# Moving a query convolution and its chunk products ahead of a block inverse, and keeping that inverse by columns

## The chip, the cores and the metric

One core of one Trainium2 chip runs the whole kernel. The metric is the device time of one execution in microseconds; three executions of the kernel before took 2511.12, 2511.8 and 2515.66 us, median 2511.8 us.

## The reference, cut to what matters

Two transformer blocks follow each other over 1024 tokens of width 1024. The first one normalizes x, projects it with `w_in`, and from the projection feeds a windowed attention and a bidirectional gated delta rule (4 heads of 128, two directions). The second block is untouched by the change. What the change touches is the front of the delta rule:

```python
qkv = silu(centred_conv(qkv, conv_w))            # 5 taps, per channel
q, k, v = split(qkv, 3);  q, k = l2norm(q), l2norm(k)
decay = exp(where(causal, gc[:, None] - gc[None, :], -inf))
kk    = einsum("cd,sd->cs", k, k)
a_mat = where(strict, beta[:, None] * kk * decay, 0)
t_mat = solve_triangular(eye + a_mat, eye)       # the inverse
qk    = einsum("cd,sd->cs", q, k) * decay
```

A serial scan over chunks then uses `t_mat`, `qk`, keys and values in each direction.

## The kernel before, in words

All matrix products of the first block keep fp32 accuracy by splitting both operands into a high and a low part and running three products (`mm3`, lines 147 to 149). Weights come in through `raw` (3 buffers), are split by ACT and POOL (lines 98 and 99) into `wh` and `wl` (8 buffers each). The kernel leaves the order of the instructions on each engine to a planner at build time, which starts from the order of the program and its own estimate of times; at run time every engine and every DMA queue works strictly in that order. SP issues the loads (`dma`), ACT issues the stores (`put`).

The order of the program, around the change:

- Lines 261 to 267 normalize eight row tiles of 128 tokens. Each tile is loaded (`hx`), scaled by DVE (line 180), transposed by PE (line 183) and split into `XN` (lines 186, 187). Tiles 0 to 3 make the first half of the tokens, 4 to 7 the second.
- Lines 351 to 356 make the 16 gate columns for each half (line 355), and lines 363 to 399 turn them into the gates `G`; the running sums go to `gc_d` in DRAM.
- `project(c0, epi)` multiplies `XN` with 512 columns in two groups of 256. It holds four weight pairs a group, so the next group is loaded while one is used. Its epilogue for keys, queries and values is `conv_epi`: both halves of 128 channels are collected in a tile `cv` (4 buffers), then for each half four or five DVE taps (lines 292, 294), a sigmoid (lines 156 to 159) and a product on POOL (line 297); the result is stored to `gk_d`, `gq_d` or `gv_d`.
- Line 412 projects the keys. Lines 415 to 424 make the decay of each of 8 chunks in a tile `e` (2 buffers), from a broadcast load of `gc_d`, and store it to `e_d`.
- Lines 431 to 456, for each chunk: load the keys (`kT`), transpose them (line 435), multiply keys with keys (line 448), load `e` back, form `b` (line 454) and store it to `key_d`.
- Lines 459 to 478, for each direction: load the 32x32 diagonal blocks `U` of all 32 chunk-heads and invert them on DVE by 31 pairs of a product (line 473) and a sum (line 475). The product reads the finished part of `X` transposed, so that its inner step is 32 elements. The inverses go to `inv_d`.
- Line 480 projects attention's keys and values, line 502 the values, lines 503 to 511 transpose them by chunk. Line 512 projects the queries and lines 513 to 524 load `kT`, `qT` and `e` again for each chunk, multiply keys with queries (line 517) and store the decayed product to `qry_d`.
- Lines 552 to 668 are the scan: `invert` widens the inverses to 128x128, `advance` runs the states of both directions. It stands before lines 670 and 671, the projections of attention's queries and of z, and before the attention (lines 677 to 737). The planner puts these products between the steps of the scan.

Of the kernel before, what the change touches and what calls it, by code (L numbers as in the profile page):

```python
# [9 lines left out]
F32 = mybir.dt.float32  # L10
# [7 lines left out]
P = 128  # L18
T = 1024
# [37 lines left out]
def tile_hybrid_layers(ctx, tc, a, out):  # L57
# [19 lines left out]
    def scratch(name, shape):  # L77
        return dr.tile(shape, F32, name=name, tag=name)
# [82 lines left out]
    def rstd_of(halves):  # L161
        st = sm.tile([P, 8], F32, name="st", tag="st")
        for j in range(2):
            act.activation(junk, halves[j], AF.Square, accum_out=st[:, j : j + 1])
        return rstd_from(st)
# [37 lines left out]
    line_d, wide_d = scratch("line_d", [8, 512]), scratch("wide_d", [8, P, 512])  # L203
    gc_d, eg_d = scratch("gc_d", [64, P]), scratch("eg_d", [64, P])
    kv_d = scratch("kv_d", [8, 2, P, 512])
    e_d = scratch("e_d", [8, 2, P, 512])

    xbq_d = [[scratch(f"{n}{d}_d", [8, 4, P, P]) for d in range(2)] for n in ("inv", "key", "qry")]

# [19 lines left out]
    def bank():  # L229
        return pg.tile([P, 512], F32, name="g", tag="g")  # L230
# [27 lines left out]
    XU = units(xp, "xn")  # L258
    XN = kts(XU)
    wb = ip.tile([P, T], F32, name="wb", tag="U", bufs=2)  # L260
    for i in range(8):
        hx = cvp.tile([P, T + 4], F32, name="cv", tag="cv")[:, :T].rearrange("p (j c) -> p j c", j=2) if 0 < i < 5 else up_tile("e", 2)
        hv = [hx[:, j, :] for j in range(2)]
        dma(hx, a["x"][0][i * P : (i + 1) * P, :].rearrange("p (j c) -> p j c", j=2))
        if i == 0:
            dma(wb, a["norm_mix_w"][0].partition_broadcast(P))
        to_units(hv, rstd_of(hv), i, wb, XU, [bank(), bank2()])


    cur = {}  # L270
# [65 lines left out]
    raw = wp.tile([P, 512], F32, name="raw", tag="raw", bufs=3)  # L336
    dma(raw[:, 0:P].rearrange("p (k m) -> p k m", k=8), W1[:, 2816:2832].rearrange("(k p) m -> p k m", p=P))

    WAB = wp.tile([P, 512], F32R, name="wh", tag="wh", bufs=8)[:, 0 : 2 * P].rearrange("p (k s m) -> p k s m", k=8, s=2)
    split(WAB[:, :, 0], WAB[:, :, 1], raw[:, 0:P].rearrange("p (k m) -> p k m", k=8), gp)  # L340
    cr = tmp()
    dma(cr[:60, 0:P], a["conv_w"][0].rearrange("t (j p) -> (t j) p", p=P))
# [66 lines left out]
    def by_head(x):  # L409
        return x.rearrange("p (h c) -> p h c", h=4)  # L410

    project(1280, conv_epi(1, gk_d))


    for c in range(8):
        e = up_tile("e", 2)
        g4 = gc_d.rearrange("(d c h) t -> c d (h t)", d=2, c=8)[c]
        dma(e, g4.partition_broadcast(P))
        for d in range(2):
            for h in range(4):  # L420
                dve.scalar_tensor_tensor(e[:, d, hs(h)], e[:, d, hs(h)], G["gc"][:, d, c, h : h + 1], neg[d],
                                         op0=ALU.subtract, op1=ALU.min)
            act.activation(e[:, d], e[:, d], AF.Exp)
        put(e_d[c].rearrange("d i j -> i d j"), e)


    z4 = ip.tile([P, P], F32, name="z4")
# [1 line left out]
    for d in range(2):  # L429
        dma(xbq_d[0][d].rearrange("c h i j -> i (c h) j"), z4.unsqueeze(1).to_broadcast([P, 32, P]))  # L430
    for c in range(8):
        kT = chunk_of(gk_d, c, "kT")
        ps = bank()
        for h in range(4):
            pe.transpose(ps[:, hs(h)], kT[:, hs(h)], ident)
        kt = up_tile("kt")
        act.copy(kt, ps)
        put(kv_d[c, 0], kt)
        for h in range(4):
            act.activation(junk[:, 0:P], kt[:, hs(h)], AF.Square, accum_out=SS[:, c, h : h + 1])  # L440
        dve.tensor_scalar(SS[:, c], SS[:, c], EPS, None, op0=ALU.add)
        dve.reciprocal(R2[:, c], SS[:, c])
        gp.tensor_tensor(NR[:, c], SS[:, c], phalf.to_broadcast([P, 4]), op=ALU.pow)
        for d in range(2):
            dve.tensor_mul(G["br"][:, d, c], G["beta"][:, d, c], R2[:, c])
        kk = bank2()
        for h in range(4):
            pe.matmul(kk[:, hs(h)], kT[:, hs(h)], kT[:, hs(h)], start=True, stop=True)
        e = up_tile("e", 2)
        dma(e, e_d[c].rearrange("d i j -> i d j"))  # L450
        b = up_tile("b", 2)
        for d in range(2):
            for h in range(4):
                dve.scalar_tensor_tensor(b[:, d, hs(h)], kk[:, hs(h)], G["br"][:, d, c, h : h + 1], e[:, d, hs(h)],
                                         op0=ALU.mult, op1=ALU.mult)
            put(xbq_d[1][d][c].rearrange("h i j -> i h j"), by_head(b[:, d]))


    for d in range(2):
        U = ip.tile([P, 32, 32], F32, name="U", tag="U", bufs=2)  # L460
        X = ip.tile([P, 32, 32], F32, name="X", tag="X", bufs=2)
        M = ip.tile([P, 31, 31], F32, name="M", tag="M", bufs=2)
        for b in range(4):
            r = slice(32 * b, 32 * b + 32)
            dma(U[r], xbq_d[1][d].rearrange("c h i j -> (c h) i j")[:, r, r])
        dve.tensor_scalar(U, U, -1.0, None, op0=ALU.mult)
        gp.memset(X, 0.0)
        gp.memset(X.rearrange("p i j -> p (i j)")[:, 0:1024:33], 1.0)
        for s in range(1, 32):
            i = 31 - s if d == 0 else s  # L470
            r = slice(i + 1, 32) if d == 0 else slice(0, i)
            m = M.rearrange("p a b -> p (a b)")[:, : s * s].rearrange("p (a b) -> p a b", a=s)
            dve.tensor_tensor(m, U[:, i, r].unsqueeze(1).to_broadcast([P, s, s]),
                                             X[:, r, r].rearrange("p j c -> p c j"), op=ALU.mult)
            dve.tensor_reduce(X[:, i, r], m, axis=AX.X, op=ALU.add)
        for b in range(4):
            r = slice(32 * b, 32 * b + 32)
            dma(xbq_d[0][d].rearrange("c h i j -> (c h) i j")[:, r, r], X[r])

    dense(W1, 512, 2, XN, kv_epi, by_half=True)  # L480

# [16 lines left out]
        act.copy(t, ps)  # L498
        put(zs_d[m * P : (m + 1) * P, h * 512 : (h + 1) * 512], t)

    PV, PQ, PZ, PA = (1792, conv_epi(2, gv_d)), (768, conv_epi(0, gq_d)), (2304, z_epi), (0, q_epi)
    project(*PV)
    for c in (0, 7, 1, 6, 2, 5, 3, 4):
        vT = chunk_of(gv_d, c, "kT")
# [4 lines left out]
        for h in range(4):  # L509
            act.activation(t[:, hs(h)], ps[:, hs(h)], AF.Copy, scale=NR[:, c, h : h + 1])  # L510
        put(kv_d[c, 1], t)
    project(*PQ)
    for c in (0, 7, 1, 6, 2, 5, 3, 4):
        kT, qT = chunk_of(gk_d, c, "kT"), chunk_of(gq_d, c, "qT")
        ps = bank2()
        for h in range(4):
            pe.matmul(ps[:, hs(h)], kT[:, hs(h)], qT[:, hs(h)], start=True, stop=True)
        e = up_tile("e", 2)
        dma(e, e_d[c].rearrange("d i j -> i d j"))
        for d in range(2):  # L520
            for h in range(4):
                dve.scalar_tensor_tensor(e[:, d, hs(h)], ps[:, hs(h)], G["br"][:, d, c, h : h + 1], e[:, d, hs(h)],
                                         op0=ALU.mult, op1=ALU.mult)
            put(xbq_d[2][d][c].rearrange("h i j -> i h j"), by_head(e[:, d]))
    s1.close()

    s2 = ctx.enter_context(ExitStack())
# [745 lines left out]
```

## Time and profile before

| | us |
|---|---|
| median of three executions | 2511.8 |
| profiled execution, its own time | 2522.66 |
| span from its first to its last instruction | 2520.9 |
| PE busy | 2384.3 (95%) |
| DVE busy | 1285.9 (51%) |
| ACT busy | 1074.3 (43%) |
| POOL busy | 928.8 (37%) |

The profiled execution is 10.9 us longer than the median. PE is TensorE's matrix work, PEld its weight loads, DVE VectorE, ACT ScalarE, POOL GpSimd, SP SyncE. Times in the rows count from the first instruction; an entry in square brackets is the idle time of the engine before the instruction and what ended it.

### The profile page before, as it was taken

The page shows a single profiled execution, that of the slowest core. Times are in us where ns is not written, and L with a number is a line of the kernel's source. Part 1 is how long each engine was busy: PE and PEld are TensorE (multiplying, and loading weights), DVE is VectorE, ACT ScalarE, POOL GpSimd, SP SyncE. Part 2 cuts the span into 40 slices and gives each one's busy share as a digit, 9 for nine tenths or more (in the row PEclk, how much of TensorE's full clock was granted, in tenths as well). Part 3 has the DMA queues.
Part 4 walks back from the last instruction along what each step waited for, and adds up shares of the span by engine and source line. Part 5 has one row for each costly group of instructions (what it writes and reads, how often), then busy time and mean ns, then how long its engine had stood idle before and what let it go on. Part 6 is the DMA issues. An engine that isn't in the chain of part 4 may idle for free. (4 is left out here: it accounts for less than half of the span.)

```text
span 2520.9 us, 31629 instructions
## 1 busy us (share of the span) xinstructions
PE 2384.3 (95%) x11098; PEld 1954.2 (78%) x11098; DVE 1285.9 (51%) x2481; ACT 1074.3 (43%) x2185; POOL 928.8 (37%) x799
## 2 busy tenths in 40 slices
PE   7899888899999999999999999998999999999998
PEld 5677677887788888888888788777777787888887
DVE  5579936885632211221123504999888885312113
ACT  5554215664542233223224423666555575333331
POOL 3344224434332222222223214455444442345354
PEclk9999988999999999999999999999999999999999
DMA  5895795656221111111112324122222225312123
GB/s 164 226 286 170 214 289 159 195 150 203 73 69 57 42 43 51 50 50 51 50 51 92 103 89 121 57 76 66 66 67 64 71 80 171 113 51 84 51 72 121
DMA packets 307282, 268.47 MB, mean 106 GB/s; under 512 B 44871, under 2 KB 240387, under 8 KB 307123
## 3 DMA queue, kind: packets, MB, share of 16 engines
q1 hardware_dynamic: 264403, 213.41, 29.6%
q10 hardware_dynamic: 42720, 53.05, 6.1%
q8 instruction: 87, 1.43, 0.2%
q14 instruction: 72, 0.59, 0.1%
HBM read 203.92 MB, written 64.57 MB: 107 GB/s over the span
## 5 line engine op out<-in xcount | busy, mean ns | idle before, releaser
L99 POOL TENSOR_TENSOR wl<-raw,wh 128x512 fp32r<-128x512 f32 x276 | 370.8, 1355 | 834.8 <-ACT wh L98 808.9
L147 PE MATMUL mm<-uh,wh 128*128 128x512 f32 x1472 | 578.3, 393 | 0.2 <-DVE mx L1066 0.2
L149 PE MATMUL mm<-uh,wl 128*128 128x512 f32 x1472 | 576.9, 392 | 0.0
L148 PE MATMUL mm<-ul,wh 128*128 128x512 f32 x1472 | 576.4, 392 | 0.0
L98 ACT CAST wh<-raw 128x512 fp32r<-128x512 f32 (+1 forms) x277 | 169.9, 618 | 460.9 <-PE mm L149 239.3
L149 PEld LDWEIGHTS mm<-uh,wl 128*128 128x128 f32 x1472 | 277.7, 189 | 59.5
L147 PEld LDWEIGHTS mm<-uh,wh 128*128 128x128 f32 x1472 | 278.1, 189 | 55.0 <-DVE mx L1066 0.6
L148 PEld LDWEIGHTS mm<-ul,wh 128*128 128x128 f32 x1472 | 277.8, 189 | 55.4
L99 DVE TENSOR_TENSOR hid<-t,hid 128x512 fp32r<-128x512 f32 x64 | 55.4, 866 | 310.1 <-ACT hid L98 310.1
L149 PE MATMUL mm<-wh,hid 128*128 128x512 f32 x512 | 199.0, 389 | 0.0
L148 PE MATMUL mm<-wl,hid 128*128 128x512 f32 x512 | 198.8, 389 | 0.0
L147 PE MATMUL mm<-wh,hid 128*128 128x512 f32 x512 | 198.7, 389 | 0.0
L845 DVE TENSOR_TENSOR h<-h,mm 128x512 f32<-128x512 f32 x128 | 87.9, 687 | 212.3 <-PE mm L149 212.2
L1015 POOL TENSOR_TENSOR ul<-u,uh 128x512 fp32r<-128x512 f32 (+3 forms) x96 | 106.1, 1106 | 134.5 <-DVE uh L1014 108.5
L147 PE MATMUL mm<-xnh,wh 128*128 128x512 f32 x352 | 142.6, 405 | 11.1 <-ACT cv L280 5.8
L110 POOL TENSOR_TENSOR wl<-raw,wh 128x512 fp32r<-128x512 f32 x72 | 101.6, 1411 | 120.7 <-DVE wh L109 45.2
L148 PE MATMUL mm<-xnl,wh 128*128 128x512 f32 x352 | 141.8, 403 | 0.0
L149 PE MATMUL mm<-xnh,wl 128*128 128x512 f32 x352 | 141.4, 402 | 0.0
L148 PEld LDWEIGHTS mm<-wl,hid 128*128 128x128 f32 x512 | 96.1, 188 | 20.0
L147 PEld LDWEIGHTS mm<-wh,hid 128*128 128x128 f32 x512 | 96.1, 188 | 20.0
L149 PEld LDWEIGHTS mm<-wh,hid 128*128 128x128 f32 x512 | 96.1, 188 | 19.9
L830 ACT ACTIVATE t<-mm 128x512 f32<-128x512 f32 x64 | 38.2, 597 | 149.8 <-PE mm L149 149.8
(331 smaller groups left out, 4616.3 us busy)
## 6 DMA issues: line engine op xcount, KB each, us to landing
raw<-in_w_in SPq DMA_DIRECT2D x172, 256.0 KB
raw<-in_w_ffn_in SPq DMA_DIRECT2D x64, 256.0 KB
raw<-in_w_ffn_out SPq DMA_DIRECT2D x64, 256.0 KB
e<-e_d SPq DMA_DIRECT2D x16, 512.0 KB
raw<-in_w_out SPq DMA_DIRECT2D x32, 256.0 KB
kv<-kv_d SPq DMA_DIRECT2D x16, 512.0 KB
kT<-gk_d SPq DMA_DIRECT2D x30, 256.0 KB
raw<-in_w_branch SPq DMA_DIRECT2D x24, 256.0 KB
```

The costliest lines, as they stand in the source:

```text
L98: act.copy(H, src)
L99: (eng or dve).tensor_sub(L, src, f32(H))
L110: gp.tensor_sub(L, raw, f32(H))
L147: pe.matmul(ps, A[0][:, asl], B[0][:, bsl], start=first, stop=False)
L148: pe.matmul(ps, A[0][:, asl], B[1][:, bsl], start=False, stop=False)
L149: pe.matmul(ps, A[1][:, asl], B[0][:, bsl], start=False, stop=last)
L830: act.activation(t, ps, AF.Relu)
L845: dve.tensor_add(Hs[order[p], n], Hs[order[p], n], ps)
L1015: gp.tensor_sub(uL[:, cs], u[:, cs], f32(uH[:, cs]))
```

## The change

The first four norms come first; then the keys' weights are loaded, both groups at once (8 pairs), and four key products over the first half of the tokens alternate with norms 4 to 7. The key products over the second half follow the gates, and the query projection follows them. The store and the two loads of `e_d` are gone: the decay of a chunk is made one chunk ahead, used for `b`, then overwritten by the key-query product. The query chunk loop is merged into the key chunk loop. The inverse keeps `X` transposed: the product reads `X` in its stored order, the sum writes a column, and an ACT copy (`Xr`) turns the result at the end. `M` and `Xr` share two buffers.

```diff
-    for i in range(8):
-        hx = ... if 0 < i < 5 else up_tile("e", 2)
+    def first_norm(i):
+        hx = ... if 0 < i < 4 else up_tile("e", 2)
...
+    for i in range(4):
+        first_norm(i)
...
-    WAB = wp.tile([P, 512], F32R, name="wh", tag="wh", bufs=8)[...]
+    WAB = gates.tile([P, 8, 2, 16], F32R, name="WAB")
...
+    GK = [cols(W1, 1280 + 256 * j, 2) for j in range(2)]
+    k_conv = conv_epi(1, gk_d)
+    def key_part(j, m, h):
+        ps = acc512()
+        for k in range(8):
+            mm3(ps, GK[j](k, m), XN[k][h], k == 0, k == 7)
+        k_conv(2 * j + m, h, ps)
     for h in range(2):
+        if h:
+            for j in range(2):
+                for m in range(2):
+                    key_part(j, m, 0)
+                    first_norm(4 + 2 * j + m)
         ps = acc512()
...
-    project(1280, conv_epi(1, gk_d))
-    for c in range(8):
+    for j in range(2):
+        for m in range(2):
+            key_part(j, m, 1)
+    project(768, conv_epi(0, gq_d))
+    def decay(c):
         e = up_tile("e", 2)
...
-        put(e_d[c].rearrange("d i j -> i d j"), e)
+        return e
+    decays = {0: decay(0)}
...
     for c in range(8):
-        kT = chunk_of(gk_d, c, "kT")
+        kT, qT = chunk_of(gk_d, c, "kT"), chunk_of(gq_d, c, "qT")
...
-        e = up_tile("e", 2)
-        dma(e, e_d[c].rearrange("d i j -> i d j"))
+        e = decays.pop(c)
+        if c < 7:
+            decays[c + 1] = decay(c + 1)
...
+        kq = bank3()
+        for h in range(4):
+            pe.matmul(kq[:, hs(h)], kT[:, hs(h)], qT[:, hs(h)], start=True, stop=True)
+        for d in range(2):
+            for h in range(4):
+                dve.scalar_tensor_tensor(e[:, d, hs(h)], kq[:, hs(h)], G["br"][...], e[:, d, hs(h)], ...)
+            put(xbq_d[2][d][c].rearrange("h i j -> i h j"), by_head(e[:, d]))
...
-        M = ip.tile([P, 31, 31], F32, name="M", tag="M", bufs=2)
+        M, Xr = (ip.tile([P, 32, 32], F32, name=n, tag="M", bufs=2) for n in ("M", "Xr"))
...
-            dve.tensor_tensor(m, U[:, i, r]..., X[:, r, r].rearrange("p j c -> p c j"), op=ALU.mult)
-            dve.tensor_reduce(X[:, i, r], m, axis=AX.X, op=ALU.add)
+            dve.tensor_tensor(m, U[:, i, r]..., X[:, r, r], op=ALU.mult)
+            dve.tensor_reduce(X[:, r, i], m, axis=AX.X, op=ALU.add)
+        act.copy(Xr, X.rearrange("p j i -> p i j"))
...
-            dma(xbq_d[0][d]...[:, r, r], X[r])
+            dma(xbq_d[0][d]...[:, r, r], Xr[r])
...
-    project(*PQ)
-    for c in (0, 7, 1, 6, 2, 5, 3, 4):
-        (kT, qT, e loads, key-query product, decayed product, store)
```

## Rows read from the trace of the kernel before

**Rows 1.** By stretch: length, PE, PEld, DVE, ACT, POOL busy (x), clock, DMA share, GB/s.

```profile
20.00:40.00 20.00, 13.54 (x57) 8.45 (x58) 17.15 (x24) 10.67 (x24) 10.89 (x12) 0.80 0.44 125
40.00:80.00 40.00, 40.00 (x174) 30.87 (x173) 18.43 (x43) 18.20 (x39) 9.73 (x12) 0.97 0.64 177
80.00:130.00 50.00, 39.48 (x166) 31.69 (x165) 26.09 (x69) 25.38 (x47) 16.43 (x17) 0.90 0.77 200
130.00:200.00 70.00, 67.52 (x325) 53.50 (x324) 55.75 (x174) 36.92 (x115) 28.00 (x29) 1.00 0.96 279
...
359.00:382.00 23.00, 13.37 (x74) 12.48 (x72) 1.55 (x4) 5.71 (x11) 14.28 (x14) 0.70 1.09 294
```

**Rows 2.** Costliest groups on PE from 20 to 39 us, with idle before them.

```profile
L183 PE MATMUL g<-ident,t 128*128 128x128 f32 x32 | 5.9, 331 | 6.2 <-DVE t L180 6.2
```

**Rows 3.** Timeline of POOL (weight splits) and of PE (first key product).

```profile
24.97 1.28 POOL L99 TENSOR_TENSOR wl<-raw,wh 128x512 fp32r<-128x512 f32 x1
...
39.04 0.63 PE L147 MATMUL mm<-xnh,wh 128*128 128x512 f32 x1
```

**Rows 4.** Timeline of PE, the three long waits from 80 to 130 us.

```profile
98.90 0.50 PE L147 MATMUL mm<-xnh,wh 128*128 128x512 f32 x1 [3.08 <-ACT cv L280]
...
108.31 0.50 PE L147 MATMUL mm<-xnh,wh 128*128 128x512 f32 x1 [2.01 <-ACT tq L309]
...
123.81 1.09 PE L435 MATMUL g<-ident,kT 128*128 128x128 f32 x4 [5.43 <-DMA kT<-gk_d]
```

**Rows 5.** Groups on DVE from 40 to 136 us: the decay.

```profile
L421 DVE SCALAR_TENSOR_TENSOR e<-e,Ggc,masks 128x128 f32<-128x128 f32 x64 | 18.3, 353 | 25.0 <-DMA e<-gc_d 24.9
```

**Rows 6.** Groups on PE from 39 to 359 us: projections and key-query products.

```profile
L147 PE MATMUL mm<-xnh,wh 128*128 128x512 f32 x352 | 142.6, 405 | 11.1 <-ACT cv L280 5.8 <-ACT t L304 3.3 <-ACT tq L309 2.0
...
L517 PE MATMUL g<-qT,kT 128*128 128x128 f32 x64 | 10.0, 310 | 3.4 <-DVE e L522 1.8 <-DMA qT<-gq_d 1.5
```

**Rows 7.** Groups on DVE from 193 to 323 us: the inverse, a convolution tap, the query product.

```profile
L473 DVE TENSOR_TENSOR M<-U,X 128x1 f32<-128x1 f32 (+30 forms) x62 | 53.9, 905 | 0.0
L475 DVE TENSOR_REDUCE X<-M 128x1 f32<-128x1 f32 (+30 forms) x62 | 28.4, 497 | 0.1
L294 DVE SCALAR_TENSOR_TENSOR gi<-cv,cw,gi 128x512 f32<-128x512 f32 x30 | 22.6, 755 | 0.0
L522 DVE SCALAR_TENSOR_TENSOR e<-g,Gbr,e 128x128 f32<-128x128 f32 x40 | 10.9, 341 | 0.0
```

**Rows 8.** Timeline of DVE: the inverse's last pair.

```profile
319.48 1.95 DVE L473 TENSOR_TENSOR M<-U,X 128x961 f32<-128x961 f32 x1
321.47 1.15 DVE L475 TENSOR_REDUCE X<-M 128x31 f32<-128x961 f32 x1
```

**Rows 9.** Page: a contiguous two-input DVE product, and the ACT copies of a weight.

```profile
L98 ACT CAST wh<-raw 128x512 fp32r<-128x512 f32 (+1 forms) x277 | 169.9, 618 | 460.9 <-PE mm L149 239.3
...
L845 DVE TENSOR_TENSOR h<-h,mm 128x512 f32<-128x512 f32 x128 | 87.9, 687 | 212.3 <-PE mm L149 212.2
```

**Rows 10.** Timelines of ACT's, SP's queue and DVE: one turn of an `e` tile.

```profile
109.81 0.38 ACTq L424 DMA_DIRECT2D e_d<-e  x1
...
116.14 0.37 SPq L418 DMA_DIRECT2D e<-gc_d  x1
...
122.89 2.33 DVE L421 SCALAR_TENSOR_TENSOR e<-e,Ggc,masks 128x128 f32<-128x128 f32 x8 [5.40 <-DMA e<-gc_d]
```

**Rows 11.** Timelines of ACT's queue and DVE: last store of `b`, first use of `U`.

```profile
184.16 0.46 ACTq L456 DMA_DIRECT2D key_d<-b  x1
...
193.97 0.69 DVE L466 TENSOR_SCALAR U<-U 128x1024 f32<-128x1024 f32 x1 [2.77 <-DMA U<-key_d]
```

**Rows 12.** Timelines of PE and ACT at the head of the scan.

```profile
337.97 1.00 PE L570 MATMUL gi<-ut,B 128*128 128x64 f32 x8
...
366.20 1.97 PE L589 MATMUL gi<-ut,B 128*128 128x64 f32 x8 [6.34 <-ACT ut L592]
...
365.77 0.37 ACT L592 COPY ut<-gi 128x256 f32<-128x256 f32 x1 [3.96 <-DMA kT<-gk_d]
```

More of the change, by code (lines that the diff above doesn't have):

```diff
@@ L205, in tile_hybrid_layers @@
     kv_d = scratch("kv_d", [8, 2, P, 512])
-    e_d = scratch("e_d", [8, 2, P, 512])
     xbq_d = [[scratch(f"{n}{d}_d", [8, 4, P, P]) for d in range(2)] for n in ("inv", "key", "qry")]
@@ L260, in tile_hybrid_layers @@
     wb = ip.tile([P, T], F32, name="wb", tag="U", bufs=2)
-    for i in range(8):
-        hx = cvp.tile([P, T + 4], F32, name="cv", tag="cv")[:, :T].rearrange("p (j c) -> p j c", j=2) if 0 < i < 5 else up_tile("e", 2)
+    def first_norm(i):
+        hx = cvp.tile([P, T + 4], F32, name="cv", tag="cv")[:, :T].rearrange("p (j c) -> p j c", j=2) if 0 < i < 4 else up_tile("e", 2)
         hv = [hx[:, j, :] for j in range(2)]
@@ L337, in tile_hybrid_layers @@
     dma(raw[:, 0:P].rearrange("p (k m) -> p k m", k=8), W1[:, 2816:2832].rearrange("(k p) m -> p k m", p=P))
-    WAB = wp.tile([P, 512], F32R, name="wh", tag="wh", bufs=8)[:, 0 : 2 * P].rearrange("p (k s m) -> p k s m", k=8, s=2)
+    WAB = gates.tile([P, 8, 2, 16], F32R, name="WAB")
     split(WAB[:, :, 0], WAB[:, :, 1], raw[:, 0:P].rearrange("p (k m) -> p k m", k=8), gp)
@@ L456, in tile_hybrid_layers @@
             put(xbq_d[1][d][c].rearrange("h i j -> i h j"), by_head(b[:, d]))
+        kq = bank3()
[3 more added lines that the diff above has]
+            for h in range(4):
+                dve.scalar_tensor_tensor(e[:, d, hs(h)], kq[:, hs(h)], G["br"][:, d, c, h : h + 1], e[:, d, hs(h)],
+                                         op0=ALU.mult, op1=ALU.mult)
+            put(xbq_d[2][d][c].rearrange("h i j -> i h j"), by_head(e[:, d]))
     for d in range(2):
@@ L472, in tile_hybrid_layers @@
             m = M.rearrange("p a b -> p (a b)")[:, : s * s].rearrange("p (a b) -> p a b", a=s)
-            dve.tensor_tensor(m, U[:, i, r].unsqueeze(1).to_broadcast([P, s, s]),
-                                             X[:, r, r].rearrange("p j c -> p c j"), op=ALU.mult)
-            dve.tensor_reduce(X[:, i, r], m, axis=AX.X, op=ALU.add)
+            dve.tensor_tensor(m, U[:, i, r].unsqueeze(1).to_broadcast([P, s, s]), X[:, r, r], op=ALU.mult)
+            dve.tensor_reduce(X[:, r, i], m, axis=AX.X, op=ALU.add)
+        act.copy(Xr, X.rearrange("p j i -> p i j"))
         for b in range(4):
             r = slice(32 * b, 32 * b + 32)
-            dma(xbq_d[0][d].rearrange("c h i j -> (c h) i j")[:, r, r], X[r])
+            dma(xbq_d[0][d].rearrange("c h i j -> (c h) i j")[:, r, r], Xr[r])
     dense(W1, 512, 2, XN, kv_epi, by_half=True)
@@ L499, in z_epi @@
         put(zs_d[m * P : (m + 1) * P, h * 512 : (h + 1) * 512], t)
-    PV, PQ, PZ, PA = (1792, conv_epi(2, gv_d)), (768, conv_epi(0, gq_d)), (2304, z_epi), (0, q_epi)
+    PV, PZ, PA = (1792, conv_epi(2, gv_d)), (2304, z_epi), (0, q_epi)
     project(*PV)
@@ L511, in tile_hybrid_layers @@
         put(kv_d[c, 1], t)
-    project(*PQ)
-    for c in (0, 7, 1, 6, 2, 5, 3, 4):
[L514 to L524, printed above, removed]
     s1.close()
```

## Prediction

> **What bounds the kernel now.** I read the busy time by stretch first [rows 1], then PE's groups and timeline in the stages the change touches [rows 2 to 6], then DVE's groups around the inverse [rows 7 to 9], then the transfers between them [rows 10, 11], and last the head of the scan [rows 12]. The page has PE busy for 2384.3 of 2520.9 us, so the kernel is bound by PE, and a change that leaves PE's products alone can only give back idle time and slow clock. This change removes no product. The reader is to see where that time is [rows 1]: from 20 to 40 us PE idles 6.5 us at a mean granted clock of 0.80. From 40 to 80 us it is full: 174 instructions in 40 us, 0.23 us each. From 80 to 130 us it idles 10.5 us at 0.90, from 130 to 200 us 2.5 us, and from 359 to 382 us 9.6 us at 0.70. Behind 660 us nothing is touched. So some 35 us of loss lie within reach, and the question is how much of it goes and what new waits appear.
>
> **The change, part by part.** The sum is made against the profiled execution, 2522.66 us; the median, 2511.8 us, is 10.9 us lower, and the result is carried over to it by the difference.
>
> *Half-token key products among the norms.* Between 20 and 39 us PE waits 6.2 us for DVE's scaled tiles [rows 2], in its strict order, while the fourth weight pair has been ready since 26.3 us and the first key product starts only at 39.04 us [rows 3]. Now the four key products over the first half, 96 matrix instructions or 22 us at 0.23 us, stand among norms 4 to 7. They need only norms 0 to 3. Their cover is the eight weight pairs, at 1.28 us each on POOL [rows 3], 10 us in all. I take -6 us. The bounds are 0 (weights or x late, since SP now loads weights ahead of four x tiles) and -9 (the part at half clock goes as well).
>
> *Eight pairs held.* All eight weight buffers stay taken until half of the second-half key products are done. Those leave 48 instructions, 11 us, in which ACT and POOL must split the queries' first pairs. Four pairs are 4 x 1.28 us on POOL plus 0.62 us on ACT [rows 3, 9], 5.7 us, so it fits if neither is blocked. I take +2 us, between 0 and +6, the whole split in the open. The gates' weights in a tile of their own cost nothing: the same split, another place.
>
> *Decay out of the keys' convolution.* PE waits 3.08 us and 2.01 us for ACT copies and 5.43 us for `kT`, 10.5 us together [rows 4]. What was late is one engine further back: DVE stood 24.9 us at the decay waiting for broadcast loads of `gc_d` [rows 5], with the convolution's taps queued behind it; ACT stood behind DVE, and PE behind ACT. After the change at most two decays stand there, and 192 query products, 45 us, cover the keys' way through DRAM. I take -10 us, between -10.5 and -5.
>
> *The query products' waits.* The 3.4 us in front of the query product and the 3.3 us in front of projections whose ACT epilogue (line 304) stood behind its stage [rows 6] leave that place: -6 us, between -6.7 and -2. Next late there is the values' way through DRAM, which stays.
>
> *The merged loop's own waits.* PE's key product, key-query product and transposes stand in one order, and the key-query product has one PSUM buffer. The nearest rows are the same waits at their old place, 3.4 us for 8 chunks [rows 6]; with a second product a chunk I take +5 us, between +2 and +12, all of the keys' 10.5 us coming back and a little more. SP's queue is in this too: the `qT` loads move ahead of the weights of everything that covers the loop, and a `qT` that waits for the query store holds those weights up.
>
> *When the scan can start.* This decides whether PE runs out of products. Before, the inverse ended at 322.6 us [rows 8], the scan's first matrix instruction came at 337.97 us [rows 12], 15 us later, and the dense products lasted to 359 us. Now: the first-half keys run from about 27 us, with 8 us of transposes and 4 us of gate columns between and behind them to about 62 us; the second half takes 22 us more, to 84 us, the queries 45 us, to 129 us. A query half costs DVE five passes of 0.755 us [rows 7] and a short one, 4.2 us, less than PE's 5.6 us, so the last one is stored near 145 us, and the first key-query product is through DVE near 159 us. From there an `e` tile must be stored, loaded, decayed and used twice. The turn of a tile before has 6.3 us from the store to the next load, 6.8 us from that to DVE, 2.3 us of decay [rows 10]. Two exponentials take 1.3 us (0.62 us each by the ACT copy of the same 512 elements, rows 9), and 16 products at 0.341 us [rows 7] take 5.5 us. That is 22 us a turn; two tiles make 11 us a chunk. Six more chunks end near 225 us, the last `b` a little later, and from the last store of `b` to `U` took 9.8 us [rows 11]: the inverse starts near 237 us, against 194 us.
>
> *The inverse by columns.* The product took 905 ns x 62 = 56 us, the sum 497 ns x 62 = 31 us [rows 7]. At 961 elements the product took 1.95 us and the sum, which reads the same 961 in stored order, 1.15 us [rows 8]; a product of 512 stored elements took 0.687 us [rows 9], 1.29 us scaled to 961. Contiguous reads should thus cost 1.15 to 1.29 us in place of 1.95 us. I take 35 us for the 62 products, -21 us, so 66 us of inverse. The values' convolution (8 halves, 34 us) shares DVE with it: the loop's six chunks of 24 products, 50 us, leave it some 25 us of 75, so about 10 us remain, and the second direction, which now follows the first since `M` and `Xr` share two buffers, ends near 313 us; the ACT copy of 1024 elements adds 2 x 0.62 us [rows 9]. The scan starts near 330 us. PE's products, moved up by the terms so far, end near 344 us. So the scan still starts 14 us before they end (before: 21 us), the first direction some 35 us sooner still.
>
> *Head of the scan.* In the stretch from 359 to 382 us the 6.34 us wait stood behind an ACT copy that ended 3.96 us of waiting for a transfer [rows 12], at a DMA share of 1.09 [rows 1]. The e loads and query stores that ran there are gone from it. I take -5 us of the 9.6 us of idle time and about 4 us of slow clock, between 0 and -14.
>
> **The sum:** -6 +2 -10 -6 +5 -5 = -20 us: 2502.7 us for a profiled execution, 2491.8 us against the median; I say 2492.
>
> **The rivals.**
>
> *The stage is bound by transfers.* The DMA share is 0.96 from 130 to 200 us and 1.09 from 359 to 382 us [rows 1]; 24 transfers of 512 KB to and from `e_d` and 8 key loads of 256 KB go, 14 MB or 50 us at 279 GB/s [rows 1]. Against it: in the first of these stretches PE was still busy for 67.5 of 70 us. If transfers set the head of the scan, the whole 14 us go there and some 3 us of the loop's waits: -32 us, 2480. Chance 0.12. The Trainium skill (Perfetto Trace Analysis, What "DMA-bound" means) has a kernel bound by DMA where the DMA engines themselves are; taken for those two stretches, it gives this rival, and the busy PE of the first speaks against it.
>
> *Little is gained.* The norms' stage stays as it is because the weights come late, and the loop's waits reach +12 us: -20 +6 +7 = -7 us, 2505. Chance 0.17.
>
> *The columns don't speed DVE up* (the change doesn't do what it says): the product is slow by its second operand, not by its order, or the written column costs as much. The inverse ends 21 us later, the scan starts 7 us after PE's products end, and the head's 5 us stay: -8 us, 2504. Against it: 512 stored elements of two operands run at nearly the sum's rate [rows 8, 9]. Chance 0.08. The Trainium skill (Advanced Engine Details and Errata, SBUF Cachelines) says that accesses which go to a new 16-byte line each time pay a penalty; by that the transposed read was the cause and this rival falls, though the written columns pay it too; the traces so far show a slow transposed read (1.95 us), no written column.
>
> *The two `e` tiles hold the inverse back* (slower). `b` of chunk c+2 now waits for the query product of chunk c, hence for the whole query convolution. Each further us a chunk moves the scan by 6 us; the margin of 14 us is gone at 13.3 us a chunk. At 18 us, where the two tiles' turns hardly overlap, the scan starts 28 us after PE's products end, and the head gains nothing: -15 + 28 = +13 us, 2525. For it: DVE was blocked 24.9 us by exactly such loads [rows 5]. Against it: even the turn before, late by 5.40 us of DVE's waiting, comes to 22 us with both products in it [rows 10], and two tiles share it. Chance 0.13.
>
> **How the numbers follow.** The forecast has 0.50, the others 0.12, 0.17, 0.08 and 0.13. About 0.2% (5 us) is about what a measurement of this kernel can tell from no change. Half of "little is gained" and a bit of the columns' case fall within it: same 0.10, slower 0.13, faster 0.77. The range holds 8 in 10: it leaves out the lower part of the transfers' case below and the bulk of the slower case above, 2476 to 2516; the sum's bounds reach from -38 to +11 us, but not all at once.
>
> **What would show it.** Right: key products before 30 us and PE idle below 2 us from 20 to 40 us; no wait of DVE for `gc_d` before 120 us; chunk period near 11 us; the product of 961 elements at 1.2 to 1.3 us; the inverse done by 313 us; dense products to about 344 us. Wrong: a PE gap of over 10 us between the projections' end and the scan, or query projections waiting for weights.

## The result, and the profile after

The changed kernel takes 2497.54 us (median of 4 runs, 2496.71 to 2500.10), the kernel before 2512.85 us beside it (2511.12 to 2515.66): 0.9942 of the time, interval 0.9929 to 0.9955, 15.3 us less. Once more in other rounds it gave 2496.97 us and 0.9939 (0.9917 to 0.9960). The profiled execution took 2500.10 us, its span is 2498.3 us; before it was 2522.66 and 2520.9 us, so the two profiles differ by 22.6 us, which is what the stretches below add up to. That is 7.3 us more than the medians differ by: the profiled execution before lies 9.8 us above the median beside it, the one after 2.6 us, and which stretch holds this surplus isn't known.

The windows of the changed kernel, on the stretches of [rows 1] and on to 700 us (columns: stretch, its length, busy time of PE, PEld, DVE, ACT and POOL with instructions, granted clock of PE, DMA share, GB/s):

```profile
20.00:40.00 20.00, 20.00 (x90) 13.92 (x89) 13.50 (x19) 9.27 (x22) 10.02 (x9) 1.00 0.49 143
40.00:80.00 40.00, 39.64 (x183) 30.45 (x182) 22.76 (x43) 19.70 (x43) 10.21 (x12) 1.00 0.20 57
80.00:130.00 50.00, 48.32 (x217) 38.28 (x216) 38.79 (x65) 27.92 (x54) 23.98 (x25) 1.00 0.65 195
130.00:200.00 70.00, 65.97 (x324) 53.99 (x323) 51.89 (x157) 35.05 (x95) 27.21 (x27) 0.98 0.75 218
200.00:260.00 60.00, 53.68 (x249) 43.14 (x248) 52.74 (x155) 26.28 (x66) 18.78 (x15) 0.97 0.83 225
260.00:320.00 60.00, 57.36 (x256) 46.13 (x255) 54.54 (x105) 24.01 (x57) 15.20 (x11) 0.97 0.61 190
320.00:360.00 40.00, 19.94 (x83) 17.18 (x83) 23.20 (x40) 14.08 (x27) 18.10 (x15) 0.66 0.81 217
360.00:420.00 60.00, 48.09 (x325) 43.80 (x323) 40.91 (x129) 37.92 (x100) 23.09 (x22) 0.89 0.52 144
420.00:560.00 140.00, 130.41 (x939) 119.53 (x939) 103.84 (x296) 83.63 (x200) 51.21 (x51) 0.95 0.68 187
560.00:700.00 140.00, 137.20 (x728) 113.87 (x727) 89.69 (x152) 70.54 (x139) 60.53 (x51) 1.00 0.43 131
```

The first three lines are what was hoped for: PE idle 0.0 us from 20 to 40 us (6.5 before) and 1.7 us from 80 to 130 us (10.5 before), at full clock in both. The line from 320 to 360 us is the price: PE idles 20.1 us there and runs at a mean clock of 0.66, where before it idled 1.0 us. The timeline of PE shows the hole:

```profile
327.07 0.39 PE L149 MATMUL mm<-xnh,wl 128*128 128x512 f32 x1
341.17 0.58 PE L721 MATMUL mm<-KH,Q 128*128 128x256 f32 x1 [13.71 <-POOL Q L716]
...
349.51 1.94 PE L590 MATMUL gi<-ut,B 128*128 128x64 f32 x8 [5.79 <-DVE sa L734]
```

The dense products end at 327.5 us (359 before); the next work is a little of attention's first block at 341.17 us, and the scan's first matrix instruction comes at 349.51 us, later than the 337.97 us of [rows 12]. Of the 22.0 us between, PE idles 19.6. The DVE timeline shows the end of the inverses:

```profile
332.86 1.16 DVE L506 TENSOR_TENSOR M<-U,X 128x961 f32<-128x961 f32 x1
334.05 1.16 DVE L507 TENSOR_REDUCE X<-M 128x31 f32<-128x961 f32 x1
...
348.53 0.71 DVE L580 STREAM_TRANSPOSE ut<-X 128x512 f32<-128x512 f32 x1 [3.33 <-DMA X<-inv_d]
```

The 961-element product takes 1.16 us, 1.95 before [rows 8]; yet the second direction ends at 335.2 us, not earlier than the 322.6 us before. From there to the scan's first matrix instruction it is another 14.3 us, for ACT's copy `Xr`, its store and the load of the scan's `X`. The copy could start at 335.2 us, but on ACT it stands behind attention's cast of `KR`, and that one waits for its load:

```profile
336.31 1.04 ACT L98 CAST KH<-KR 128x1024 fp32r<-128x1024 f32 x1 [6.92 <-DMA KR<-ka_d]
338.04 0.62 ACT L715 CAST Q<-R 128x512 fp32r<-128x512 f32 x1 [0.69 <-DMA R<-qa_d]
338.56 1.94 ACT L508 COPY Xr<-X 128x1024 f32<-128x1024 f32 x1
```

So attention's early place, which fills 2.5 us of the hole, also holds this copy up by 3.4 us. The copy alone doesn't decide the scan's start: in e8 below it ends at 333.8 us, and the scan starts at 349.8 all the same.

**One ledger for all runs.** Lost time here is PE's idle time plus half of its busy time at the lower level of the granted clock (0.5, 1.2 GHz), worked out from the trace's clock records. What is left of a span is PE's work at full clock; it is 2350.4 us before, 2344.1 us after, and 2341.5 to 2347.1 us in the eleven other profiles below (each span minus its lost time), so lost time tells the kernels apart down to some 5 us. One profiled execution, e2's, ran at a mean granted clock of 0.596 for 3971.7 us, and nothing is read from it. Before, lost time was 55.9 us up to 320 us, 54.6 us from 320 to 700 us and 60.0 us behind; after, it is 32.3, 61.5 and 60.4 us. A second profile of the changed kernel (e12) has 30.6, 56.6 and 59.9 us: so much two profiles of one kernel differ.

### The profile page after: what moved, and what is told of

It reads as the page before. It is cut to its first block, busy times and chain, and to the rows that moved or that the text cites. A ratio compares the mean times of both kernels' runs of the same rounds, so it can differ in the third digit from the quotient of the medians.

```text
span 2498.3 us, 31498 instructions
## 1 busy us (share of the span) xinstructions
PE 2376.8 (95%) x11098; PEld 1954.1 (78%) x11098; DVE 1281.5 (51%) x2481; ACT 1079.9 (43%) x2187; POOL 928.1 (37%) x799
## 5 line engine op out<-in xcount | busy, mean ns | idle before, releaser
L98 ACT CAST wh<-raw 128x512 fp32r<-128x512 f32 x276 | 169.9, 619 | 449.6 <-PE mm L149 234.2
```

The lines of the kernel that those rows point to most:

```text
L98: act.copy(H, src)
```

## The experiments

Theory A: the time falls by the idle and half-clock time that each part sheds, part by part. Theory B: it follows the start of the scan. Theory C: attention fills the hole whatever the inverses do. Later ones are D (the order on SP's queue) and E (below). All ran in 5 rounds against the kernel before, whose medians beside them were 2511.0 us (e1 to e4), 2511.9 (e5 to e8), 2512.5 (e9 to e11) and 2511.0 (e12). Lost time, in us, comes from one profile of each. e12 is the changed kernel's repeat.

| run | us | ratio to before, interval | lost to 320 | lost 320 to 700 | attention's first product | scan's first |
|---|---|---|---|---|---|---|
| before (profile of rows 1) | | 1 | 55.9 | 54.6 | 381.9 | 338.0 |
| changed | 2497.54 | 0.9942 (0.9929, 0.9955) | 32.3 | 61.5 | 341.2 | 349.5 |
| e1 only half-token keys | 2518.99 | 1.0026 (1.0015, 1.0037) | 49.2 | 59.5 | 379.1 | 347.5 |
| e2 only the loop | 2513.89 | 1.0011 (1.0000, 1.0022) | | | | |
| e3 only columns | 2508.33 | 0.9987 (0.9973, 1.0001) | 44.3 | 58.5 | 374.7 | 339.7 |
| e4 changed, by rows | 2513.69 | 1.0012 (0.9998, 1.0025) | 31.3 | 77.9 | 374.1 | 345.6 |
| e5 same, directions in turn | 2512.44 | 1.0004 (0.9994, 1.0015) | 37.6 | 65.1 | 349.4 | 361.0 |
| e6 changed, directions together | 2502.86 | 0.9961 (0.9949, 0.9974) | 33.8 | 63.9 | 361.7 | 333.8 |
| e7 changed, norms first | 2493.68 | 0.9925 (0.9908, 0.9942) | 33.8 | 57.9 | 340.0 | 348.2 |
| e8 changed, four e tiles | 2514.12 | 1.0009 (0.9995, 1.0022) | 35.3 | 70.5 | 343.2 | 349.8 |
| e9 changed, no loop | 2521.62 | 1.0035 (1.0019, 1.0052) | 38.7 | 72.8 | 348.0 | 353.6 |
| e10 changed, whole key products | 2514.06 | 1.0005 (0.9991, 1.0018) | 40.2 | 60.3 | 348.5 | 353.9 |
| e11 e6, attention's loads on ACT | 2503.55 | 0.9961 (0.9945, 0.9977) | 34.7 | 63.2 | 356.7 | 338.2 |
| e12 changed, again | 2496.97 | 0.9939 (0.9917, 0.9960) | 30.6 | 56.6 | 339.5 | 347.6 |

### One part at a time

e1 is the kernel before with these lines of the diff alone:

```diff
+    for i in range(4):
+        first_norm(i)
+                    key_part(j, m, 0)
+                    first_norm(4 + 2 * j + m)
-    project(1280, conv_epi(1, gk_d))
+            key_part(j, m, 1)
```

> The kernel before with one part alone: half-token key products among norms 4 to 7, eight weight pairs held. Theory A (the time falls by the idle time and slow clock that PE sheds upstream, part by part): PE idles under 1 us from 20 to 40 us, the dense products end some 8 us sooner, and the time falls by 6 to 9 us. Theory B (the time follows the start of the scan alone, which hangs on DVE's chain through decay, b and inverse): the keys' products start 12 us sooner, but the decay's waits hold DVE, so the scan starts as before, within 3 us, and the time moves by less than 3 us.

Measured: 1.0026 of the time, some 7 us slower. The part itself does what was said (first key product at 20.9 us, no idle time from 20 to 40 us), but from 80 to 130 us PE is still busy for only 42.76 of 50 us (39.48 before), and `U` is ready at 226.7 us instead of 194: with the decay and the queries where they were, 6.7 us less are lost up to 320 us and 9.5 us more behind. No theory had it slower.

e2 has the queries behind the keys and the merged loop with its decay, and nothing else:

```diff
-        put(e_d[c].rearrange("d i j -> i d j"), e)
+    project(768, conv_epi(0, gq_d))
+        e = decays.pop(c)
+            pe.matmul(kq[:, hs(h)], kT[:, hs(h)], qT[:, hs(h)], start=True, stop=True)
```

> The kernel before with one part alone: query projection behind the keys, decay kept on chip, merged chunk loop; inverse by rows, norms and keys as before. Theory A: the three waits of PE from 80 to 130 us (10.5 us) and the query products' waits go, the dense products end 10 to 15 us sooner; the inverse, by rows, ends 25 to 40 us later than before, so a hole opens in front of the scan that takes 20 to 30 us: the time rises by 5 to 15 us. Theory B: the scan starts 25 to 40 us later and the time rises by all of it, 25 to 40 us. Rival C (the hole is filled by the attention): the time falls by 10 us.

Measured: 1.0011, some 3 us slower. The time is just below what A expected (its interval reaches 5.5 us, A's range begins at 5), and rules out B and C; where it arises isn't seen, as there is no profile to read.

e3 has the columns alone (`X[:, r, r]` read in stored order, `Xr`):

```diff
-            dve.tensor_tensor(m, ..., X[:, r, r].rearrange("p j c -> p c j"), op=ALU.mult)
-            dve.tensor_reduce(X[:, i, r], m, axis=AX.X, op=ALU.add)
+            dve.tensor_tensor(m, ..., X[:, r, r], op=ALU.mult)
+            dve.tensor_reduce(X[:, r, i], m, axis=AX.X, op=ALU.add)
+        act.copy(Xr, X.rearrange("p j i -> p i j"))
```

> The kernel before with one part alone: the inverse by columns with the ACT copy. The 62 products fall from 56 to about 39 us, the inverse ends 12 to 20 us sooner. Theory A: the dense products still end near 359 us, the scan starts sooner inside them, and the time falls by 0 to 5 us, what the head of the scan (9.6 us idle) gives. Theory B: the time falls with the scan's start, by 12 to 20 us.

Measured: 0.9987, some 3 us faster, and not clear of no change. The products fall from 56.1 to 42.8 us, but the two directions now run one after the other and end at 328.2 us (322.6 before), so the scan is no sooner. The time lies in A's range, but not for A's reason, and B's condition, an earlier scan, wasn't reached.

Alone the three parts come to +7, +3 and -3 us of some 2512, together to -15. e4 undoes the columns in the changed kernel (the last diff read backwards):

> The changed kernel with the inverse by rows again, everything else kept. The products cost 17 us more on DVE, the dense products still end near 327 us, and the scan starts some 17 us later than 349.5 us. Theory A and B alike: the hole grows and the time rises by 10 to 17 us against the changed kernel. Rival C (attention and output products fill the hole): less than 4 us.

Measured: 1.0012 against 0.9942, so the columns are worth 0.70%, 17 us, here. C falls. A and B both expected that size, but the profile fits neither: the scan starts at 345.6 us, 4 us before the changed kernel's. What comes later is attention, at 374.1 us instead of 341.2. PE's timeline in that run:

```profile
345.65 1.73 PE L589 MATMUL gi<-ut,B 128*128 128x64 f32 x7 [19.87 <-DMA B<-key_d]
```

Nothing fills the hole before the scan. On SP's queue the stores of both directions stand together, then the scan's loads, then attention's. In the changed kernel SP's timeline has attention's loads ahead of the second direction's stores:

```profile
327.92 0.39 SPq L700 DMA_DIRECT2D bias<-wide_d  x1
328.35 1.15 SPq L704 DMA_DIRECT2D KR<-ka_d  x2
329.55 1.32 SPq L713 DMA_DIRECT2D R<-qa_d  x2
...
340.53 2.69 SPq L511 DMA_DIRECT2D inv_d<-Xr  x4
343.31 1.76 SPq L713 DMA_DIRECT2D R<-qa_d  x2
345.17 0.55 SPq L577 DMA_DIRECT2D X<-inv_d  x1
```

That gave theory D: it is the order, not the speed.

### Speed against order

e5 and e6 cross the two. e5 has rows with the directions in turn, e6 columns with the directions together:

```diff
e5 against e4:
-        M = ip.tile([P, 31, 31], F32, name="M", tag="M", bufs=2)
+        M = ip.tile([P, 31, 31], F32, name="M", tag="M", bufs=1)
e6 against the changed kernel:
-        M, Xr = (ip.tile([P, 32, 32], F32, name=n, tag="M", bufs=2) for n in ("M", "Xr"))
+        M = ip.tile([P, 32, 32], F32, name="M", tag="M", bufs=2)
+        Xr = U
         act.copy(Xr, X.rearrange("p j i -> p i j"))
```

> The changed kernel with the inverses by rows again (961-element products at 1.95 us in place of 1.16), but with one buffer for the product tile, so that direction 1 follows direction 0 as it does in the changed kernel, and SP's queue holds attention's bias, KR and R loads between the two directions' stores. Theory D (the 16 us of the columns come by the place of attention's loads on SP's queue): attention's first product at 338 to 346 although direction 1 ends some 17 us later than in the changed kernel (350 to 355), and 2497 to 2505 us, ratio to the kernel before 0.994 to 0.998. Theory A (the DVE time saved by the contiguous read): no better than the rows with both directions together, 2511 to 2520, ratio 1.000 to 1.004. Theory B (the start of the scan): the scan starts at 363 to 368, 15 us later than changed, 2512 to 2516.

> The changed kernel with the turned copy of X written over U, so that both directions have a product tile and run between each other; all eight stores of the inverses and the scan's first loads then stand ahead of attention's bias, KR and R on SP's queue. Theory D: attention's first product not before 350, and the gain of the columns mostly lost though the inverse ends sooner (318 to 328): 2505 to 2514 us, ratio 0.998 to 1.001. Theory A (DVE time) and theory B (start of the scan, here at 328 to 338, 10 to 20 us sooner than changed): 2480 to 2497 us, ratio 0.988 to 0.994.

Measured, with ratios to before:

| | directions together, scan's loads first | in turn, attention's loads first |
|---|---|---|
| rows | e4 1.0012 | e5 1.0004 |
| columns | e6 0.9961 | changed 0.9942 |

From the upper line to the lower the read in stored order is worth 0.51% and 0.62% (13 and 16 us); from left to right the order is worth 0.08% and 0.19% (2 and 5 us), within the intervals. So D falls, and so does B: in e6 the scan starts 15.7 us sooner than in the changed kernel and the time is 5 us longer; in e5 it starts 15.4 us later than in e4, and the ratios agree. e6's ratio lies in no theory's range, between D's (0.998 to 1.001) and that of A and B (0.988 to 0.994), and e5's attention started at 349.4 us, not at 338 to 346, so D's condition was reached in part only. What the speed does can be read in starts: at the same order the scan comes 11.8 us sooner (345.6 to 333.8) and 11.5 us (361.0 to 349.5), attention 12.4 and 8.2 us. The windows of e6 also show what the hole costs when it is short:

```profile
320.00:360.00 40.00, 29.38 (x126) 25.98 (x124) 7.59 (x14) 9.92 (x18) 12.52 (x16) 0.66 1.01 264
...
332.00:358.00 26.00, 19.25 (x82) 18.11 (x83) 5.42 (x12) 2.54 (x5) 6.04 (x11) 0.50 1.08 296
```

PE idles only 10.6 of these 40 us (20.1 in the changed kernel), but the clock is 0.50 from 332 to 358 us all the same, behind a gap of 4.96 us; with PE busy for longer at that clock, the half clock costs 10.1 us from 332 to 359 us, against 5.7 in the changed kernel.

e11 takes e6 and issues attention's first loads on ACT's queue:

```diff
-        dma(bias, ...)
-            dma(KR[64 * s : 64 * s + 64], ...)
+        (put if kv == 0 else dma)(bias, ...)
+            (put if kv == 0 else dma)(KR[64 * s : 64 * s + 64], ...)
```

(and the first two `R` loads in the same way).

> Both directions of the columns' inverse together, as in the run of that name, but attention's first bias, KR and first two R loads are issued on ACT's queue, so that they don't stand behind the scan's loads on SP's. If the 5 us by which that run lost to the changed kernel come by attention's late start (theory D in its small form): attention's first product at 338 to 350, the scan still from 332 to 337, 2493 to 2499 us, ratio 0.992 to 0.995. If attention's products only take the place of later ones (theory B, or a fixed sum of work): attention's start moves, the time doesn't, 2501 to 2505, ratio 0.996 to 0.997.

Measured: 0.9961, as e6. Attention moved by 5 us only, to 356.7 us: on ACT the `KR` loads stand behind the first copy of the scan, which waits for PE until 340.19 us. The time agrees with D's rival; D's condition (338 to 350 us) wasn't reached.

### The other parts undone

e7 has all norms first, with the products still by halves; e8 four `e` tiles and the turned copy on DVE:

```diff
e7:
-    for i in range(4):
+    for i in range(8):
         first_norm(i)
-                    first_norm(4 + 2 * j + m)
e8:
-        e = up_tile("e", 2)
+        e = up_tile("e", 2) if c % 4 < 2 else ip.tile([P, 2, 512], F32, name="e4", tag="M", bufs=2)
-        act.copy(Xr, X.rearrange("p j i -> p i j"))
+        dve.tensor_copy(Xr, X.rearrange("p j i -> p i j"))
```

> The changed kernel with all eight norms ahead of the keys' products, as the kernel before had them; the products stay half-token ones. By the prediction's term (idle and half-speed time before the first key product): PE idle 20 to 40 us back at some 6 us, 6 to 9 us slower than the changed kernel, 2503 to 2507, ratio 0.997 to 1.000. By the rival that the part alone showed (it made the kernel before 8 us slower by what the planner did later): no slower, 2490 to 2498, ratio 0.989 to 0.994.

Measured: 0.9925, not slower than the changed kernel (the intervals overlap). PE idles 1.1 us from 20 to 40 us, and the first key product stands at 20.8 us: the norms' new place gives nothing that is seen here, and the half-token products give the whole gain of that stretch, since they need norms 0 to 3 alone wherever the others are issued. It is the fastest kernel of the study by its median, but not shown to be faster than the changed one.

> The changed kernel with four e tiles in place of two (two of them in the inverse's product buffers) and the turned copy on DVE. If the wait of a decay's load for the query product two chunks before sets the loop (12.5 us a chunk, DVE waiting 2.7 to 4.6 us on the e load): DVE's waits on the e load under 1 us, 10 to 11 us a chunk, U ready 8 to 14 us sooner (233 to 238), the scan 8 to 14 us sooner (336 to 341), the hole on PE after the dense products shorter by as much. Theory D, with attention's loads still ahead of direction 1's stores: 0 to 6 us faster than the changed kernel, 2491 to 2498, ratio 0.991 to 0.994, since attention already fills the hole. Theory B: 2483 to 2490, ratio 0.988 to 0.991. If the loop is limited by something else (POOL, ACT): U no sooner, no change.

Measured: 1.0009, 17 us slower than the changed kernel, and `U` is no sooner: 248.8 us (246.3). But the chunks do come faster. The `b` of the third and of the eighth chunk, and the windows between them, in the changed kernel and then with four tiles:

```profile
172.60 2.16 DVE L478 SCALAR_TENSOR_TENSOR b<-g,Gbr,e 128x128 f32<-128x128 f32 x8
...
235.31 2.15 DVE L478 SCALAR_TENSOR_TENSOR b<-g,Gbr,e 128x128 f32<-128x128 f32 x8
...
172.60:235.30 62.70, 55.35 (x274) 45.85 (x273) 54.14 (x179) 31.76 (x90) 21.01 (x18) 0.95 0.85 229
```

```profile
183.78 2.15 DVE L478 SCALAR_TENSOR_TENSOR b<-g,Gbr,e 128x128 f32<-128x128 f32 x8
...
238.56 2.15 DVE L478 SCALAR_TENSOR_TENSOR b<-g,Gbr,e 128x128 f32<-128x128 f32 x8
...
183.80:238.60 54.80, 47.99 (x241) 39.61 (x239) 49.28 (x164) 27.71 (x81) 20.16 (x17) 0.94 0.84 245
```

That is 12.5 us a chunk with two tiles (12.4 to 12.6 in the seven other profiles that have this loop with two tiles) and 11.0 with four; in these stretches DVE waits 8.5 and 3.3 us for the `gc_d` loads of `e`. So the number of tiles seems to cost some 1.5 us a chunk, and DVE's own work, 10.8 and 9.9 us a chunk, lies close below either pace. `U` is no sooner because the third chunk begins 11.2 us later. The 17 us come mostly later (70.5 us lost between 320 and 700 us, 61.5 and 56.6 in the changed kernel's two profiles) in code that the edit hardly touches: the planner orders everything anew, and which part of that order costs the time wasn't found. The run holds two edits, and neither was run alone.

e9 undoes the loop (e1 and e3 together), e10 the half-token keys with their norms (e2 and e3 together):

> The kernel before with the half-token key products and the inverses by columns, without the merged loop (queries first, decay written out and read back, as before). If the parts simply add (half-token keys alone +8, columns alone -2.6): 2515 to 2520 us, ratio 1.001 to 1.004. If what counts is PE's idle and half-speed time round the start of the scan, where a part helps only when the dense products' end and the inverses' end both move (theory E): dense products end at 336 to 342, the scan starts at 342 to 352, idle between them under 12 us, 2503 to 2511 us, ratio 0.996 to 1.000.

> The changed kernel with all norms first and the keys' products over all tokens at once, as before; merged loop and inverses by columns stay. If the parts add (loop alone +3, columns alone -2.6): 2510 to 2514 us, ratio 0.999 to 1.001. By theory E and the prediction's term (6.5 us of idle and some 5 us of half speed between 20 and 40 us come back, first key product at 39 us, all else shifted by as much): 8 to 12 us slower than the changed kernel, 2505 to 2510, ratio 0.997 to 0.9995. By the rival that everything up to 130 us is hidden behind the inverses anyway: no slower than the changed kernel, 2494 to 2500.

Measured: 1.0035 and 1.0005, so taking the loop out of the changed kernel costs 0.93% (23 us) and taking out the half-token keys 0.63% (16 us). Both came out as if the parts simply added, or worse; theory E's ranges, 2503 to 2511 and 2505 to 2510 us, hold neither median, though its condition for e9 wasn't met either: the dense products end at 334.3 us, sooner than said, and the scan starts at 353.6, later. Part of each cost shows where it was expected. Windows of e9 and then of e10:

```profile
80.00:130.00 50.00, 42.90 (x182) 34.10 (x181) 27.05 (x48) 22.97 (x51) 16.83 (x17) 0.93 0.85 243
130.00:200.00 70.00, 62.31 (x299) 49.55 (x298) 61.89 (x173) 40.08 (x103) 27.51 (x31) 1.00 0.82 261
```

```profile
20.00:40.00 20.00, 13.76 (x60) 9.17 (x60) 16.68 (x28) 11.33 (x25) 11.96 (x10) 0.79 0.50 154
```

PE's idle time is back at the old places: 7.1 and 7.7 us without the loop, 6.2 us at a clock of 0.79 without the half tokens. In the ledger e9 loses 6.4 us more than the changed kernel up to 320 us, and 11.3 us more from 320 to 700 us; e10 loses 7.9 us more up to 320 us, 1.2 us less to 700 us and 3.3 us more behind. Both profiles ran faster than their medians, by 5.5 and 3.8 us, so the ledger doesn't hold all of either cost.

> The changed kernel itself once more, in the same rounds against the kernel before as the others had, since what each undone part costs is counted from it. If its 15 us are the kernel's own (theories A and E): 2494 to 2500 us, ratio 0.993 to 0.996, so that undoing the loop, the half-token keys or the columns costs 15 to 25 us each, and the run with all norms first stays no slower than it. If they came by the chip or the hour: ratio 0.997 to 1.001, and the costs of the undone parts shrink to under 10 us.

Measured: 0.9939. The changed kernel's gain is its own, and the costs of the undone parts stand as measured. They are costs of whole programs, though: every edit has the planner order everything anew, e8 lost 17 us in that way or in one not found, and no run tells a part's own work from the order that came with it.

**What follows.** Keys and loop together shed 24.6 us up to 320 us, with or without the columns (e4; 23.6 in the changed kernel). In e4 nearly all of it comes back, 23.3 us more between 320 and 700 us than before; with the columns 16.4 us of that are saved (77.9 to 61.5). Alone, the keys shed 6.7 us up to 320 us and the columns 11.6 us, yet the time is 7 us longer with the keys and 3 us shorter with the columns. A reading that fits, but that no run isolates: in e4 the dense products end at 325.8 us and DVE's inverses only at 338.3, so shedding time ahead of them leaves PE waiting, and faster inverses shorten the wait; in e3 the dense products last to 345.3 us, beyond the scan's start at 339.7. So the columns would be worth 3 us there and 13 to 17 here.

## Why the prediction was right, and where it wasn't

**The number.** 2492 us was forecast and 2497.54 measured, well inside the range; -20 us was forecast, and it is -15.3 between the medians and -22.6 between the two profiles, in which the terms are read here. Of its signs of being right, the first key product (20.9 us), the idle time from 20 to 40 us, DVE's waits for `gc_d` before 120 us (0.6 us) and the faster product came about; the pace of the chunks, the end of the inverses and that of the dense products didn't, and its sign of being wrong, a gap of PE of over 10 us before the scan, did, with 13.71 us.

**The bound.** Right: PE's work stays, only idle time and slow clock move.

**Half-token keys,** -6 us: right, and more, since the half clock went too (0.80 to 1.00), which had been kept as a bound. That they stand *among the norms* doesn't matter (e7). **Eight pairs held,** +2 us: not seen, PE idles 0.4 us from 40 to 80 us. **Decay out,** -10 us: right, 8.8 us of idle time and the half clock. Together the ledger's lost time from 20 to 130 us falls by 21.7 us (17.0 idle and 6.8 half clock before, 2.0 and none after), where -14 had been summed.

**The query products' waits and the loop's own,** -6 and +5 us: the net came out, 1.7 us less lost from 130 to 320 us, but by luck. PE's waits in that stretch before, and then after:

```profile
PE mm L147 <- ACT t L304: 3.3, 3, 2.7
PE g L507 <- DMA kT<-gv_d: 3.0, 1, 3.0
PE g L507 <- ACT kt L510: 1.8, 2, 1.4
```

```profile
PE g L458 <- DMA kT<-gk_d: 8.6, 4, 2.7
PE mm L147 <- ACT t L307: 4.1, 2, 2.6
PE g L483 <- DMA qT<-gq_d: 0.3, 1, 0.3
```

The key-query product's 3.4 us went, but the 3.3 us in front of the projections didn't leave: 4.1 us stand there. The loop's own waits became 8.9 us, nearly all for `kT` and none for the PSUM buffer. What made up for both are waits that no term counted on, above all the 4.8 us on the values' way through DRAM, which had been said to stay.

The price of a chunk was too low: 12.5 us instead of 11. As far as e8, one run with two edits, can show it, the limit was rightly sought in the turn of two tiles, since four of them bring the pace to 11.0 us; but the turn of a tile came to 25 us, not 22.

**When the scan can start.** This step failed. It said that the scan starts 14 us before the dense products end; it started 22 us after them. Three terms were mis-sized. The inverse began at 246 us, not 237, by the chunks' pace. It took 89 us, not 76; DVE's groups from 246 to 336 us show why:

```profile
L506 DVE TENSOR_TENSOR M<-U,X 128x1 f32<-128x1 f32 (+30 forms) x62 | 39.1, 631 | 1.9
L507 DVE TENSOR_REDUCE X<-M 128x1 f32<-128x1 f32 (+30 forms) x62 | 31.2, 504 | 1.9
L297 DVE SCALAR_TENSOR_TENSOR gi<-cv,cw,gi 128x512 f32<-128x512 f32 x8 | 6.0, 751 | 0.0
L498 DVE TENSOR_SCALAR U<-U 128x1024 f32<-128x1024 f32 x2 | 3.1, 1536 | 2.5 <-DMA U<-key_d 2.5
```

The products were to take 35 us and took 39.1, the convolution's and `U`'s work is 15 us where 10 had been left, and some 4 us are gaps of the chain. The products' excess isn't their own: at the smaller time that each size took in one of the two directions, all 62 come to 32.7 us, and 6.0 of the other 6.4 us are in ten single products that ran beside POOL's weight splits. From the timelines of DVE and of POOL:

```profile
302.09 0.26 DVE L506 TENSOR_TENSOR M<-U,X 128x100 f32<-128x100 f32 x1
...
302.68 1.02 DVE L506 TENSOR_TENSOR M<-U,X 128x121 f32<-128x121 f32 x1
...
302.26 3.91 POOL L99 TENSOR_TENSOR wl<-raw,wh 128x512 fp32r<-128x512 f32 x3 [19.82 <-ACT wh L98]
```

In the other direction the product of 121 elements took 0.29 us. And the dense products end at 327.5 us, not 344: 23.6 us were shed up to 320 us instead of 15, and the scan's first matrix instructions no longer stand among them. So of the 36 us between the forecast 14 us and the 22 us found, 16.5 are the products' earlier end, the price of a larger gain upstream, and 19.5 the scan's later start.

**Head of the scan,** -5 us: it became +15.9 us from 320 to 420 us (26.9 us lost before, 42.8 after). From 420 to 700 us 9 us went that no step had named (27.7 to 18.7). Why is open: attention began 40 us sooner, but it did in e8 too (343.2 us), and there 28.3 us are lost in that stretch. So: -21.7, -1.7, +15.9 and -9.0, with -6.3 us in work at full clock, +0.5 us behind 700 us and -0.2 us ahead of 20 us, make up the 22.6 us. That -20 came near it is in part luck: a term had the wrong sign, the ones upstream gave more than was summed, and 9 us came from where no term was.

**The rivals.** The transfers' case falls: from 130 to 200 us the DMA share went from 0.96 to 0.75 and PE's idle time from 2.5 to 4.0 us. *Little is gained* falls too: the norms' stage gave all it had, and the loop's waits stayed below 12 us. That the columns don't speed DVE falls by 1.95 to 1.16 us; the Trainium skill (Advanced Engine Details and Errata, SBUF Cachelines) would have the written columns pay as well, and the trace doesn't show that: the sum that writes a column takes 1.16 us, the one that wrote a row 1.15 [rows 8]. The slower case came half true: a hole of 22 us where it named 28, of which attention filled 2.5; two `e` tiles made up a part of it, at some 1.5 us a chunk, and more was gained upstream than it cost.

## What to carry to other kernels

Time that is shed ahead of a serial stage can come back as waiting in front of it, as nearly all of it did in e4: sum that stage's own chain (here DVE's loop, inverse, copy, store and load), the instructions of the engine that feeds it as well as the turns of the buffers, and what else those instructions run beside. A part that is worth little alone can be worth much more in company, so undo parts from the changed kernel as well as doing them alone. And where a planner orders the work, an edit can move the time by 17 us elsewhere, so the cost of an undone part isn't yet the worth of its own work.

## What the runs showed of the hardware

Two gaps of very different length were followed by the same stretch at half clock: 13.71 us in the changed kernel and 4.96 us in e6 both by 27.3 us at 1.2 GHz (332 to 359 us), though PE was busy for 19.25 of 26 us there in e6 and for 10.48 us in the changed kernel. In e4 37.5 us followed a gap of 19.87 us. The same window of the changed kernel, beside e6's above:

```profile
332.00:358.00 26.00, 10.48 (x43) 9.73 (x44) 10.17 (x25) 10.52 (x21) 10.14 (x10) 0.50 0.96 250
```

Some DVE products of two inputs took up to 1.1 us longer beside POOL's weight splits: 1.02 us instead of 0.29 for 121 elements, shown above, and in e8 2.24 us for 961 elements at 329.31 us, where the changed kernel's took 1.16. Not all did: in the changed kernel those from 323 to 328 us kept their time, and it was POOL's four splits that took 6.92 us, at 1.28 us each elsewhere [rows 3].

And the engine matters for a copy that turns 1024 elements: ACT took 1.94 us, where its cast of 1024 elements in stored order took 1.04 (both shown with the hole above); DVE took 1.04 us for the turned copy. So a turned read alone doesn't slow DVE as it slowed the product. From the timeline of e8:

```profile
329.31 2.24 DVE L506 TENSOR_TENSOR M<-U,X 128x961 f32<-128x961 f32 x1
...
332.77 1.04 DVE L508 COPY Xr<-X 128x1024 f32<-128x1024 f32 x1
```
